# Two of four quarters of a gate stage's input transposed by DMA in 16 bit halves instead of on TensorE

## The chip, the cores and the metric

The kernel runs on one core of a Trainium2 chip. The metric is the device time of one execution in microseconds (us); lower is better. One core has TensorE (PE in the profile: matmuls and transposes into PSUM), VectorE (DVE), ScalarE (ACT), GpSimd (POOL) and SyncE (SP, which only issues transfers here), each with its own instruction stream, and 16 DMA engines that serve all transfers.

## The reference, cut to what matters

One layer of a trunk: sliding window attention, its output projection added to x, then a gate computed from the normed x.

```python
hn = rmsnorm(x, norm_g[0])
y = swa_mixer(hn, w_in, w_out, sinks, rel_bias)   # ends in (out * silu(gate)) @ w_out
x = x + y
emb = p[0] @ ple_proj[0]
g = sigmoid(rmsnorm(x, ple_norm[0]) @ ple_gate[0])
x = x + emb * g
return rmsnorm(x, final_g)
```

Sequence 512, width 2048, float32 throughout; `w_out` and `ple_gate` are 2048x2048, the p input is 512x256.

## The kernel before, in words

The span falls into projections and attention (to 452 us), the w_out stage (452 to 607), the gate stage (607 to about 783) and a short tail. The change is in the last two.

*Products.* Both stages multiply a 512x2048 input by a 2048x2048 weight. Each is cut into 2x2 blocks and done with seven block products instead of eight (1 to 7), at the price of sums and differences: the input's are made on VectorE (`Forms`, L815 to L846), the weight's by accumulating transfers earlier in DRAM (`SUMS`) or, for two products of the gate, in place in SBUF (tiles `grown`, L707). `ORDER_OUT` and `ORDER_PLE` (L649) give the order of the products; w_out's product 2 is itself done by seven smaller products (`small`), whose pieces are put between the others by the tables `SMALL` and `small_steps`. In w_out a product's result is added to or subtracted from blocks of x, which lies in SBUF as `x1s` (`add_y`, `add_to_x`, L1031 and L1033).

*Float32 in three matmuls.* PE multiplies in a reduced format, so each operand is split in a high and a low part and a product takes three matmuls (`mm3`, L126 to L128). The weights come in *pieces* of 128x1024 (512 KB). A piece is loaded by SP (L720) into a tile `braw` or `grown`, split into `bhi` by ScalarE (L727, a cast) and `blo` by VectorE (L728, a subtraction of two SBUF tiles), and used by 12 matmuls, a small product's piece by 6. Splits are made two pieces ahead, loads three to six pieces ahead, in SP's order.

*Turning x.* The gate stage needs x with its columns on the partitions. `turn` (L1005) does it on PE: for a pair of column blocks `kp` and one half of the rows `th`, four transposes of 128x128 by an identity into a PSUM bank (L1015), and two ScalarE multiplications by the norm's gain `pn` from there into the tile `hT` (L1018), of which there are four (`hT0` to `hT3`, each four column blocks by 512 rows). With 8 values of `kp` and two halves there are 64 transposes and 32 multiplications. Twelve of the 16 turns stand in w_out's last product 4, four in the gate's first product 2. A block of x is turned after its last addition (`missing` counts them); at that moment ScalarE also sums its squares (`squares`, L1001) for the norm, whose factor is applied later.

*Order.* Up to the gate's second product a scheduler sets the order of each engine's stream; from there it is as written. Waits are between instructions, and a stream is in order: an instruction that waits holds all that stand behind it on its engine.

Of the kernel before, what the change touches and what calls it, by code (L numbers as in the profile page):

```python
# [11 lines left out]
F32 = mybir.dt.float32  # L12
F32R = mybir.dt.float32r
AF = mybir.ActivationFunctionType
# [4 lines left out]
D = 2048  # L19
# [36 lines left out]
def trunk_kernel(ctx: ExitStack, tc: tile.TileContext, a: dict):  # L56
# [587 lines left out]
    def blk(t):  # L644
# [4 lines left out]
    ORDER_OUT, ORDER_PLE = (1, 7, 6, 5, 3, 4), (2, 7, 1, 6, 5, 3, 4)  # L649

    SMALL = {
        (5, 0): {1: 1, 3: 1}, (5, 1): {1: 7, 3: 7}, (3, 0): {1: 6, 3: 6}, (3, 1): {1: 2, 3: 2},
        (4, 0): {0: 5, 1: 5, 2: 4, 3: 4}, (4, 1): {0: 3, 1: 3},
# [151 lines left out]
    far_from, far_to = at_out[6, 0][0], at_ple[ORDER_PLE[0], 0][0]  # L805

    class Forms:
# [6 lines left out]
        def steps(self, p):  # L814

            self.made[p] = []
            for h in range(2):
# [13 lines left out]
                if sub:  # L831
                    nc.vector.tensor_sub(src, *sub)
                    yield
# [116 lines left out]
    fg = late.tile([P, D], F32, name="fg")  # L950
    pTh = late.tile([P, 2, S], F32R, name="pTh")
    pTl = late.tile([P, 2, S], F32R, name="pTl")
# [5 lines left out]
    def banks(p, jj, nm):  # L958

        if p in (6, 5, 3):  # L960
            return chain[jj]
        tag = ("to" if p in (7, 2) else "sp")[jj]
        ps = [bank(f"{nm}{p}_{jj}_{tb}", tag) for tb in range(2)]
        if p == 1:
            chain[jj] = ps
        return ps

    later = []
# [6 lines left out]
    def unit(p, jj, at, forms, todo, between=lambda m: None):  # L975

        ps = banks(p, jj, forms.nm)
        f = forms.made[p]
        first = p not in (6, 5, 3)
        for m in range(4):  # L980
            bh, bl = B.get(at[p, jj][m])
            for kk in range(2):
# [21 lines left out]

    def turn(kp, th, tag):  # L1005

        g = kp // 2
        if g not in hT:
            hT[g] = quarter(f"hT{g}")
# [6 lines left out]
        for n in range(2):  # L1016
            k = 2 * kp + n
            nc.scalar.mul(hT[g][:, k % 4, th * 256 : th * 256 + 256], tp[:, n * 256 : n * 256 + 256], pn[:, k : k + 1])  # L1018

    ple_forms = Forms(hT, "g")  # L1020
    ple_first = ple_forms.steps(2)


    missing = {(j, t): {(0, 0): 1, (1, 0): 3, (0, 1): 1, (1, 1): 2}[t // 2, j // 2] for j in range(4) for t in range(NB)}
# [3 lines left out]
    def add_to_x(j, t, sign, ps):  # L1028
# [6 lines left out]
        if not missing[j, t]:  # L1035
            squares(t, j)

# [4 lines left out]
    small_forms = {}  # L1042

    def small_form(q):
# [5 lines left out]
        fh, fl = (  # L1050
            acts.tile([P, 2, 256], F32R, tag=tag, name=f"small_{tag}{q}").rearrange("p k (h t) -> p (k h) t", h=2)
            for tag in ("ah", "al")
        )
# [16 lines left out]
        (6, 1, 2): 1, (5, 0, 0): 7, (5, 0, 2): 7, (5, 1, 0): 6, (5, 1, 2): 6, (3, 0, 2): 2, (3, 1, 0): 5, (3, 1, 2): 5,  # L1070
        (3, 1, 3): 4, (4, 0, 1): 3, (4, 0, 3): 3,
# [35 lines left out]
    turns = []  # L1107


# [3 lines left out]
    waiting = {(7, 0): (1, 0), (6, 0): (1, 1)}  # L1113
    held = {}
    for n, p in enumerate(ORDER_OUT):
        nxt = out_forms.steps(ORDER_OUT[n + 1]) if n < 5 else iter(())
        for jj in range(2):
# [11 lines left out]
            def todo():  # L1129
# [19 lines left out]
        if p == 3:  # L1149
            nc.sync.dma_start(fg, a["final_g"].partition_broadcast(P))  # L1150
        if p == 3:
            turns = [(kp, th) for kp0, th in ((4, 1), (4, 0), (0, 0)) for kp in range(kp0, kp0 + 4)]
    run(ple_first)
    assert not turns
# [5 lines left out]
    nc.sync.dma_start(pT, a["pT"])  # L1160
    nc.scalar.copy(pTh, pT)
# [44 lines left out]
    s2, s7 = partial("s2"), partial("s7")  # L1206
# [253 lines left out]
```

## Time and profile before

| What | Value |
|---|---|
| Median of 3 runs | 794.84 us (793.84 to 795.72) |
| The profiled execution | 794.82 us |
| Its span in the trace | 793.1 us |
| Granted TensorE clock | 0.997 |
| PE, DVE, ACT, POOL busy | 783.2, 585.7, 506.7, 148.5 us |
| DMA | 45,066 packets, 185.23 MB |

The profile is of one execution. Its span is what the trace covers; the execution's own time has 1.72 us more around it. A group's row gives the line, the engine, what is written from what, the count, then busy time and the mean duration in ns. A matmul's row shows some 390 ns, while the next starts 227 ns after it, since they are pipelined; the chain of work counts start to start. A row of transfers gives the count, the size and the median time from issue to landing.

### The profile page before, as it was taken

Reading aid. Unit: us, or ns where it says so; the run is one execution under the profiler, and the core shown is the slowest. Engines: PE = TensorE matmul, PEld = TensorE weight load, DVE = VectorE, ACT = ScalarE, POOL = GpSimd, SP = SyncE. Lnnn points to the kernel's source line nnn. Section 1 sums busy time; section 2 is a strip of 40 time slices with the busy share of each in tenths; the row PEclk is TensorE's granted clock in tenths of the full one; section 3 lists DMA queues with packets and bytes.
Section 4 is the critical chain, followed back from the end, with each engine's and each line's share of the span. In section 5 each row is a group of like instructions: output and inputs, shape, how many; then the busy total and the mean of one; then the engine's idle time right before and its main releaser. Section 6 shows DMA issues by size and latency. Waiting matters only on the chain.

```text
span 793.1 us, 11181 instructions
## 1 busy us (share of the span) xinstructions
PE 783.2 (99%) x3746; PEld 656.0 (83%) x3746; DVE 585.7 (74%) x1155; ACT 506.7 (64%) x1067; POOL 148.5 (19%) x248
## 2 busy tenths in 40 slices
PE   9999999999999999999999999999999999999995
PEld 8888888888888888888888888888888888888885
DVE  4547587867867587767777899778866757988896
ACT  6743576666767586766666654466699656656765
POOL 0200423242413324132324200000000120210000
PEclk9999999999999999999999999999999999999998
DMA  9977999897989989898987498667864996787533
GB/s 349 275 215 264 207 275 303 223 267 215 277 227 269 223 249 258 230 247 235 244 227 182 140 365 337 197 212 232 275 237 142 346 203 202 157 225 220 176 107 106
DMA packets 45066, 185.23 MB, mean 234 GB/s; under 512 B 6656, under 2 KB 7680, under 8 KB 39888
## 3 DMA queue, kind: packets, MB, share of 16 engines
q1 hardware_dynamic: 36928, 143.30, 53.0%
q0 software_dynamic: 8080, 41.22, 27.1%
q8 instruction: 29, 0.48, 0.2%
q14 instruction: 29, 0.24, 0.1%
HBM read 177.63 MB, written 62.97 MB: 303 GB/s over the span
## 4 chain that ended last, share of the span: by engine, by line
PE 99%; DVE 0%; ACT 0%; ACTq 0%; issue 0%; DVEq 0%
PE gps L126 7%; PE gps L127 7%; PE gps L128 7%; PE qps L126 7%; PE qps L127 7%; PE qps L128 7%; PE o L127 6%; PE g L128 6%; PE g L127 5%; PE o L126 5%; PE o L128 5%; PE g L126 5%; PE s L477 2%; PE o L583 2%; PE vps L290 2%; PE pt L541 2%
## 5 line engine op out<-in xcount | busy, mean ns | idle before, releaser
L728 DVE TENSOR_TENSOR blo<-braw,bhi 128x1024 fp32r<-128x1024 f32 x102 | 124.4, 1222 | 40.9 <-ACT bhi L727 40.6
L727 ACT CAST bhi<-braw 128x1024 fp32r<-128x1024 f32 x102 | 107.3, 1052 | 72.2 <-PE o L128 24.8
L126 PE MATMUL gps<-xh,whi 128*128 128x512 f32 x256 | 100.0, 390 | 0.0
L127 PE MATMUL gps<-xl,whi 128*128 128x512 f32 x256 | 99.9, 390 | 0.0
L128 PE MATMUL gps<-xh,wlo 128*128 128x512 f32 x256 | 99.8, 390 | 0.0
L126 PE MATMUL qps<-xh,whi 128*128 128x512 f32 x224 | 87.8, 392 | 0.0
L127 PE MATMUL qps<-xl,whi 128*128 128x512 f32 x224 | 87.4, 390 | 0.0
L128 PE MATMUL qps<-xh,wlo 128*128 128x512 f32 x224 | 87.3, 390 | 0.0
L110 DVE TENSOR_TENSOR wlo<-wraw,whi 128x1024 fp32r<-128x1024 f32 x60 | 73.7, 1229 | 6.1 <-ACT whi L109 5.9
L547 DVE TENSOR_TENSOR r<-pt,r 128x256 fp32r<-128x256 f32 x64 | 27.2, 424 | 66.5 <-ACT r L546 65.6
L546 ACT CAST r<-pt 128x256 fp32r<-128x256 f32 x64 | 23.9, 373 | 80.9 <-PE pt L541 80.8
L126 PE MATMUL g<-bhi,fhg 128*128 128x512 f32 x192 | 75.1, 391 | 0.0
L126 PE MATMUL o<-bhi,fho 128*128 128x512 f32 x192 | 74.8, 390 | 0.0
L128 PE MATMUL g<-bhi,flg 128*128 128x512 f32 x192 | 74.8, 389 | 0.0
L127 PE MATMUL o<-blo,fho 128*128 128x512 f32 x192 | 74.8, 389 | 0.0
L128 PE MATMUL o<-bhi,flo 128*128 128x512 f32 x192 | 74.7, 389 | 0.0
L127 PE MATMUL g<-blo,fhg 128*128 128x512 f32 x192 | 74.7, 389 | 0.0
L557 POOL TENSOR_SCALAR_AFFINE_SELECT own<-r 64x512 fp32r<-64x512 f32 (+1 forms) x48 | 32.5, 677 | 224.6 <-DVE r L547 208.7
L109 ACT CAST whi<-wraw 128x1024 fp32r<-128x1024 f32 x60 | 62.2, 1039 | 5.4 <-issue 4.0
L492 POOL COPY t<-sinkb 128x2 f32<-128x2 f32 x64 | 53.2, 839 | 57.7 <-ACT sinkb L873 32.4
L707 POOL DMA_DIRECT2D grown<-in_ple_gate x16 | 13.8, 861 | 231.0 <-DVE blo L728 226.7
L128 PEld LDWEIGHTS gps<-xh,wlo 128*128 128x128 f32 x256 | 48.1, 188 | 10.3
(228 smaller groups left out, 1800.3 us busy)
## 6 DMA issues: line engine op xcount, KB each, us to landing
wraw<-in_w_gate_in SPq DMA_DIRECT2D x32, 512.0 KB, 6.5
w_out<-in_w_out POOLq DMA_DIRECT2D x32, 512.0 KB, 8.0
braw<-w_out SPq DMA_DIRECT2D x32, 512.0 KB, 4.4
wraw<-in_w_q SPq DMA_DIRECT2D x28, 512.0 KB, 5.3
braw<-in_ple_gate SPq DMA_DIRECT2D x24, 512.0 KB, 4.1
braw<-in_w_out SPq DMA_DIRECT2D x22, 512.0 KB, 4.2
xw<-in_first SPq DMA_DIRECT2D x14, 640.5 KB, 6.4
w_out<-in_w_out SPq DMA_DIRECT2D x16, 512.0 KB, 10.1
```

Of the source, the lines that this page charges most:

```text
L109: nc.scalar.copy(hi, raw)
L110: nc.vector.tensor_sub(lo, raw, hi.bitcast(F32))
L126: nc.tensor.matmul(ps, sh, mh, start=first, stop=False, skip_group_check=more)
L127: nc.tensor.matmul(ps, sh, ml, start=False, stop=False, skip_group_check=more)
L128: nc.tensor.matmul(ps, sl, mh, start=False, stop=last, skip_group_check=more)
L290: nc.tensor.matmul(v_ps[t], h[:, c], part_of(high_at, 256, 512), start=f, stop=e, skip_group_check=True)
L492: nc.gpsimd.tensor_copy(two(0, W + W - 1 if late else W, 1), sinkb[:, d : d + 1].unsqueeze(1).to_broadcast([P, 2, 1]))
L546: nc.scalar.copy(rh, src)
L547: nc.vector.tensor_sub(rl, src, rh.bitcast(F32))
L557: nc.gpsimd.affine_select(out=flat(own), in_=flat(r).bitcast(F32), pattern=[[0, 8], [sign, HB]], compare_op=ALU.is_ge, fill=0.0, base=-HB ...
L727: nc.scalar.copy(hi, raw)
L728: nc.vector.tensor_sub(lo, raw, hi.bitcast(F32))
```

## The change

- The two lower quarters of the rows (blocks `t` of 2 and 3, 256 of 512 rows, all columns) are no longer turned on PE. When such a block of x is complete, POOL copies it apart into its 16 bit halves (`apart`), writes them to DRAM (`halves_of`, 256 KB for each of the eight blocks), and some six pieces later (`cross`) SP issues a transposing transfer of 16 bit elements from there into `hT`, where low and high halves fall beside each other again. ScalarE then multiplies by `pn` in place.
- `turn` stays for the upper rows: 8 turns, 32 transposes. Four of them stand in w_out's last product, now 3, and four in the gate's first product, now 7.
- `ORDER_OUT` becomes (1, 7, 4, 6, 5, 3) and `ORDER_PLE` (7, 2, 1, 6, 5, 3, 4). w_out's product 4 accumulates into the banks of product 7 (with 7's sign turned), so that 7 is added to one block of x instead of two. Small products and their forms move with the order.
- The forms of the gate's products are made when the quarters that they need are there (`due`, `forward`, `finish`).
- `fg` (the last norm's gain, 1 MB) and the split p input lie in the tiles that the small products' forms leave, and are loaded later.

```diff
@@
-    ORDER_OUT, ORDER_PLE = (1, 7, 6, 5, 3, 4), (2, 7, 1, 6, 5, 3, 4)
+    ORDER_OUT, ORDER_PLE = (1, 7, 4, 6, 5, 3), (7, 2, 1, 6, 5, 3, 4)
...
-        (5, 0): {1: 1, 3: 1}, (5, 1): {1: 7, 3: 7}, (3, 0): {1: 6, 3: 6}, (3, 1): {1: 2, 3: 2},
...
+        (6, 0): {1: 1, 3: 1}, (6, 1): {0: 7, 2: 7}, (5, 0): {0: 6, 1: 6, 3: 2}, (5, 1): {0: 2, 2: 5, 3: 5},
...
-                        1: (a11, None), 7: (a11, (a21, a11)), 2: (a12, None), 6: (a11, (a22, a11)),
+                        1: (a11, None), 7: (a11, (a11, a21)), 2: (a12, None), 6: (a11, (a22, a11)),
...
-                    nc.vector.tensor_sub(src, *sub)
+                    (nc.vector.tensor_add if (self.nm, p) == ("o", 6) else nc.vector.tensor_sub)(src, *sub)
...
@@
+        if (nm, p) == ("o", 4):
+            return sevens[jj]
...
+    halves_of = [tc.dram_tile([S, 2, 512], U16, name=f"halves_of{j}") for j in range(4)]
...
+    def apart(t, j):
...
+        to = room[:, 1024 * n : 1024 * n + 1024].rearrange("p (h c) -> p h c", h=2)
+        nc.gpsimd.tensor_copy(to, x1[j][:, t, :].bitcast(U16).rearrange("p (c h) -> p h c", h=2))
+        nc.gpsimd.dma_start(halves_of[j][t * P : (t + 1) * P], to)
+        written.append((clock[0], t, j))
+
+    def cross():
+
+        clock[0] += 1
+        while crossed and crossed[0][0] <= clock[0] - 4 and (crossed[0][2] < 2 or clock[0] > 60):
+            _, th, j = crossed.pop(0)
+            for k in range(4):
+                part = hT[j][:, k, th * 256 : th * 256 + 256]
+                nc.scalar.mul(part, part, pn[:, 4 * j + k : 4 * j + k + 1])
+            scaled.add((th, j))
+        while written and written[0][0] <= clock[0] - 6 and (written[0][2] < 2 or clock[0] > 50):
+            _, t, j = written.pop(0)
+            to = turned(j).rearrange("p k t -> p (k t)").bitcast(U16).rearrange("p (k t) -> p k t", k=4)
+            nc.sync.dma_start_transpose(
+                to[:, :, t * 2 * P : (t + 1) * 2 * P], halves_of[j][t * P : (t + 1) * P].rearrange("t h c -> (t h) c")
+            )
...
+    def forward():
+
+        while ahead:
+            p, steps = ahead[0]
+            h = len(ple_forms.made.get(p, ())) // 2
+            if not scaled.issuperset({7: {(0, h), (1, h)}, 2: {(0, 2 + h)}}.get(p, ()) if h < 2 else ()):
+                return
+            if next(steps, "end") != "end":
+                return True
+            ahead.pop(0)
+        return True
...
         if not missing[j, t]:
             squares(t, j)
+            if t >= 2:
+                apart(t, j)
...
-            1: [(c11, -1)], 7: [(c22, 1), (c21, -1)], 6: [(c21, -1)], 5: [(c22, 1)], 3: [(c12, 1)],
+            1: [(c11, -1)], 7: [(c22, -1)], 6: [(c21, -1)], 5: [(c22, 1)], 3: [(c12, 1)],
...
-                if p == 4:
-
-                    for _ in range({0: 1, 1: 2, 2: 2, 3: 2, 5: 1, 6: 2, 7: 2}.get(4 * jj + step, 0)):
-                        turn(*turns.pop(0), "o")
-                    if jj:
-                        next(ple_first, None)
+                cross()
+                if p == 3 and jj:
+                    for kp in {0: (0, 1), 1: (2, 3)}.get(step, ()):
+                        turn(kp, 0, "o")
+                    forward()
...
+    finish()
+    fg = late.tile([P, D], F32, tag="two", name="fg")
+    nc.sync.dma_start(fg, a["final_g"].partition_broadcast(P))
...
+                cross()
+                if p == 7:
+                    for kp in {0: (4,), 1: (5,), 3: (6,), 4: (7,)}.get(4 * jj + step, ()):
+                        turn(kp, 0, "s")
```

Three places in the engines' streams show what has moved. A row there has the line of its kernel (the kernel after has its own numbers: L721 is L720 of before, L1065 is L1018, L1062 is L1015), the operation, and out<-in with the numbers of the tiles.

SP, before, from the end of w_out's loads into the gate stage: the pieces of the gate's product 2 (`braw` from `in_ple_gate`), the p input, and the first seeds of product 7 (`grown` from `ple_gate_7`).

```order
L720 DMA braw61_6181<-w_out_4_1_3_808 128x1024
L720 DMA braw62_6258<-in_ple_gate 128x1024
L720 DMA braw63_6270<-in_ple_gate 128x1024
L720 DMA braw64_6310<-in_ple_gate 128x1024
L1160 DMA pT_6352<-in_pT 128x1024
L720 DMA braw65_6361<-in_ple_gate 128x1024
L720 DMA braw66_6363<-in_ple_gate 128x1024
L720 DMA braw67_6391<-in_ple_gate 128x1024
L720 DMA braw68_6419<-in_ple_gate 128x1024
L720 DMA grown70_6421<-ple_gate_7_0_0_809 128x1024
L720 DMA braw69_6446<-in_ple_gate 128x1024
```

SP, after, at the start of the gate stage: the last seeds of product 7, with `fg` and the p input between them, then the transposing transfers into `hT2` and `hT3`, then the first pieces of product 2.

```order
L721 DMA grown67_6285<-ple_gate_7_1_1_814 128x1024
L1221 DMA fg_6312<-in_final_g 128x2048
L1227 DMA pT_6316<-in_pT 128x1024
L721 DMA grown68_6326<-ple_gate_7_1_2_815 128x1024
L721 DMA grown69_6355<-ple_gate_7_1_3_816 128x1024
L1045 DMA_TRANSPOSE hT2_6352<-halves_of2_5009 128x4x256 x2
L1045 DMA_TRANSPOSE hT3_6401<-halves_of3_5010 128x4x256 x2
L721 DMA braw70_6429<-in_ple_gate 128x1024
L721 DMA braw71_6472<-in_ple_gate 128x1024
```

The weights of product 2 now stand behind four transposing transfers (two in each row with x2), and these behind all seeds of product 7; the other four stand further up, behind the loads of pieces 46, 47, 51 and 52 in w_out's products 5 and 3.

ScalarE, before, in w_out's product 4: casts of pieces (`bhi`), sums of squares (`junk`), and the first evacuations of turned blocks into `hT2` and `hT3`.

```order
L727 CAST bhi49_5991<-braw49_5910 128x1024
L727 CAST bhi50_6006<-braw50_5932 128x1024
L727 CAST bhi51_6035<-braw51_5944 128x1024
L1001 ACTIVATE junk0_0_6023,ssq2_5008<-x1s_5004 128x512
L1018 ACTIVATE hT2_6025<-tp4_1_6026,pn_68 128x256 x2
L727 CAST bhi52_6047<-braw52_5967 128x1024
L1001 ACTIVATE junk3_0_6064,ssq2_5008<-x1s_5004 128x512
L727 CAST bhi53_6086<-braw53_5989 128x1024
L1018 ACTIVATE hT2_6025<-tp5_1_6066,pn_68 128x256 x2
L1018 ACTIVATE hT3_6073<-tp6_1_6074,pn_68 128x256 x2
L727 CAST bhi54_6098<-braw54_6004 128x1024
```

ScalarE, after, over pieces 42 to 47 in w_out's products 5 and 3: the in-place multiplications of `hT0` and `hT1` (L1040), which need the transposing transfers landed.

```order
L728 CAST bhi42_5841<-braw42_5762 128x1024
L1040 ACTIVATE hT0_5862<-hT0_5862,pn_68 128x256 x4
L728 CAST bhi43_5866<-braw43_5786 128x1024
L728 CAST bhi44_5889<-braw44_5798 128x1024
L1006 ACTIVATE junk2_2_5918,ssq2_5005<-x1s_5004 128x512
L728 CAST bhi45_5901<-braw45_5827 128x1024
L728 CAST bhi46_5931<-braw46_5839 128x1024
L728 CAST bhi47_5943<-braw47_5864 128x1024
L1136 CAST small_two3_6028<-small_sums_5011 128x512
L1040 ACTIVATE hT1_5966<-hT1_5966,pn_68 128x256
L1006 ACTIVATE junk0_0_5960,ssq2_5005<-x1s_5004 128x512
L1006 ACTIVATE junk2_3_5987,ssq2_5005<-x1s_5004 128x512
```

The four multiplications of `hT0` stand ahead of the cast of piece 43. Of those of `hT1`, the first comes ahead of the cast of piece 48 and the other three between the casts of 48 and 49.

POOL, after, behind the loads of x; before, the accumulations of `grown` (L707 there, L708 here) followed at once.

```order
L999 DMA x1s_5004<-in_x 128x4x512 x2
L1029 COPY apart0_5698<-x1s_5004 128x1024 x2
L1030 DMA halves_of0_5007<-apart0_5698 128x1024 x2
L1029 COPY apart0_5698<-x1s_5004 128x1024
L1030 DMA halves_of1_5008<-apart0_5698 128x1024
L1029 COPY apart0_5698<-x1s_5004 128x1024
L1030 DMA halves_of1_5008<-apart0_5698 128x1024
L1029 COPY apart4_5920<-x1s_5004 128x1024 x2
L1030 DMA halves_of2_5009<-apart4_5920 128x1024 x2
L1029 COPY apart4_5920<-x1s_5004 128x1024 x2
L1030 DMA halves_of3_5010<-apart4_5920 128x1024 x2
L708 DMA grown62_6150<-in_ple_gate 128x1024
```

Eight copies and eight writes now stand between the loads of x and the first accumulation.

More of the change, by code (lines that the diff above doesn't have):

```diff
@@ L1049, in small_form @@
         }[q]
[L1050 to L1053, printed above, removed]
+        tag, n = {1: ("one", 0), 7: ("one", 1), 6: ("two", 0), 2: ("two", 1), 5: ("one", 0), 4: ("one", 1), 3: ("two", 0)}[q]
+        if n == 0:
+            pairs[tag] = late.tile([P, 4, 512], F32R, tag=tag, name=f"small_{tag}{q}")
+        fh, fl = (pairs[tag][:, 2 * n + v].rearrange("p (k t) -> p k t", k=4) for v in range(2))
         small_forms[q] = fh, fl
@@ L1148, in trunk_kernel @@
         run(nxt)
[L1149 to L1154, printed above, removed]
+        if p == 5:
+            due(7)
+    finish()
+    fg = late.tile([P, D], F32, tag="two", name="fg")
+    nc.sync.dma_start(fg, a["final_g"].partition_broadcast(P))
     rstd2 = const.tile([P, NB], F32, name="rstd2")
@@ L1160, in trunk_kernel @@
     nc.sync.dma_start(pT, a["pT"])
+    pTs = late.tile([P, 2, 2, S], F32R, tag="one", name="pTs")
+    pTh, pTl = pTs[:, 0], pTs[:, 1]
     nc.scalar.copy(pTh, pT)
@@ L1290, in trunk_kernel @@
                 later.extend(moved.pop())
[L1291 removed]
+        if p != 7:
+            finish()
     while later:
```

85 lines of the change are left out of this document (53 added, 32 removed).

## The prediction

> **What bounds the kernel now.** I read the page first: the busy shares and the chain that ended last.
>
> ```profile
> PE 783.2 (99%) x3746; PEld 656.0 (83%) x3746; DVE 585.7 (74%) x1155; ACT 506.7 (64%) x1067; POOL 148.5 (19%) x248
> PE 99%; DVE 0%; ACT 0%; ACTq 0%; issue 0%; DVEq 0%
> ```
>
> TensorE is busy for 99% of the span and is 99% of the chain. An average can hide a stage with another limit, so next came the windows of the stages that the change touches (columns: PE, PEld, DVE, ACT, POOL busy, clock, DMA share, GB/s).
>
> ```profile
> 470.00:480.00 10.00, 10.00 (x45) 8.16 (x44) 10.00 (x12) 5.56 (x7) 0.00 (x0) 1.00 0.72 257
> 490.00:500.00 10.00, 10.00 (x45) 8.26 (x44) 8.71 (x11) 5.77 (x7) 0.00 (x0) 1.00 0.83 312
> 500.00:510.00 10.00, 10.00 (x46) 8.28 (x45) 6.14 (x7) 3.67 (x4) 0.00 (x0) 1.00 0.63 206
> 585.00:590.00 5.00, 5.00 (x29) 4.24 (x28) 3.15 (x4) 4.04 (x8) 0.00 (x0) 1.00 0.99 393
> 590.00:600.00 10.00, 10.00 (x50) 8.30 (x49) 8.96 (x11) 9.50 (x18) 0.00 (x0) 1.00 0.03 12
> 640.00:650.00 10.00, 10.00 (x46) 8.29 (x45) 5.50 (x5) 5.20 (x7) 2.79 (x4) 1.00 1.03 192
> ```
>
> PE has no gap in any of them, at full clock. So every microsecond taken off PE here comes off the end, if nothing makes PE wait; and every wait of PE is added in full. Three neighbours are close: VectorE is full at 470-480 (and eases to 6.14 of 10 by 510), ScalarE nearly so at 590-600, and the DMA engines are full at 585-590 and at 640-650. The last two differ: at 585-590 plain loads move 393 GB/s, at 640-650 a full set of engines moves 192, because only the accumulating transfers of `grown` run then.
>
> The pace of a piece of weights shows in those accumulations, each released by the split of one piece:
>
> ```profile
> 636.66 0.85 POOL L707 DMA_DIRECT2D grown<-in_ple_gate  x1 [1.87 <-DVE blo L728]
> 639.38 0.85 POOL L707 DMA_DIRECT2D grown<-in_ple_gate  x1 [1.87 <-DVE blo L728]
> ```
>
> A piece is 2.72 us of PE, and one accumulation takes that long with all engines busy.
>
> **What it removes.** Half of the 64 TensorE transposes go. The chain's longest pieces price them (start, length, what):
>
> ```profile
> 574.97 0.44 PE tp L1015 x4
> 579.53 0.87 PE tp L1015 x8
> ...
> 606.75 0.87 PE tp L1015 x8
> 610.37 0.44 PE tp L1015 x4
> 613.56 0.44 PE tp L1015 x4
> ...
> 619.95 0.44 PE tp L1015 x4
> ```
>
> There are six pieces of 4 (0.44) and five of 8 (0.87): 2.64 + 4.35 = 6.99 us for 64. What stays is two groups of 8 and four of 4: 1.74 + 1.76 = 3.50. So PE loses 6.99 - 3.50 = 3.49 us. The count of matmuls is otherwise the same: product 4 accumulates in the banks of product 7, which costs PE nothing. The bound from below is 794.82 (this execution, span 793.1 and 1.72 around it) - 3.49 = 791.33.
>
> ```profile
> L1018 ACT ACTIVATE hT<-tp,pn 128x256 f32<-128x256 f32 x32 | 12.8, 472 | 0.0
> L1033 DVE TENSOR_TENSOR x1s<-x1s,o 128x512 f32<-128x512 f32 x12 | 7.8, 681 | 0.0
> L728 DVE TENSOR_TENSOR blo<-braw,bhi 128x1024 fp32r<-128x1024 f32 x102 | 124.4, 1222 | 40.9 <-ACT bhi L727 40.6
> L727 ACT CAST bhi<-braw 128x1024 fp32r<-128x1024 f32 x102 | 107.3, 1052 | 72.2 <-PE o L128 24.8 <-PE g L128 20.0 <-DMA braw<-w_out 7.5
> ```
>
> ScalarE's 32 multiplications become 16 from PSUM and 16 in place, of the same 128x256: no change in sum. VectorE loses four additions into x, 4 x 0.68 = 2.7 us, because product 7 goes to one block of x instead of two. Nothing of this is on the chain, so it counts nothing. The new order does move VectorE's sums and additions earlier, into the full stretch that begins at 470, by some 1 us around the sixteenth piece (the changed order, summed with these durations); a wait of PE there is under 1 us, and from 490 on VectorE has the room to make it up.
>
> **What it adds on POOL.** Eight copies to 16 bit halves and eight writes of 256 KB, on an engine that does nothing in the windows from 470 to 600; behind them on POOL stand only the accumulations of `grown`, first due at the end of the w_out stage. For the copies the nearest row of the engine is the masking of 128x512.
>
> ```profile
> 110.11 0.67 POOL L557 TENSOR_SCALAR_AFFINE_SELECT own<-r 128x512 fp32r<-128x512 f32 x1 [4.58 <-DVE r L547]
> 105.34 0.18 POOL L492 COPY t<-sinkb 128x2 f32<-128x2 f32 x1
> 111.24 1.46 POOL L492 COPY t<-sinkb 128x2 f32<-128x2 f32 x1
> 111.45 1.23 DVE L110 TENSOR_TENSOR wlo<-wraw,whi 128x1024 fp32r<-128x1024 f32 x1
> x1s<-s POOLq DMA_DIRECT2D x4, 256.0 KB, 5.2
> ```
>
> For 1,024 halves that is 2 x 0.67 = 1.3 us by elements. The transposes are issued six pieces (16 us) behind the writes, and copy and write are 1.3 + 5.2 = 6.5 us, so their length is covered. What isn't: the small copy took 0.18 us alone and 1.46 us when a VectorE split of two SBUF inputs started 0.21 us in; it ended only with the split. So POOL waits for VectorE, and I must suppose the reverse: each copy can hold a split back by up to 1.3 us. A split comes 2 pieces ahead, so one delay is absorbed where VectorE has room; in a full stretch it isn't. The bounds are 0 and 8 x 1.3 = 10.4 us; I take 0.3, a quarter of one copy, since the copies begin past 500, where VectorE has room. The Trainium skill, "SBUF — State Buffer", § Who interferes with whom, holds that a VectorE instruction with two SBUF inputs and a GpSimd one that reads SBUF shut each other out for a whole instruction, whichever began first; by that the copies' price would be near the upper bound in a full stretch. The trace agrees in the one direction that it shows (1.46 against 0.18), and no row shows the other.
>
> **What it adds on SP: eight DMA transposes of 256 KB.** No row of before shows one. Call T the time for which one holds the DMA engines. From the nearest rows:
>
> ```profile
> out<-x1s SPq DMA_DIRECT2D x14, 256.0 KB, 2.8
> braw<-in_ple_gate SPq DMA_DIRECT2D x24, 512.0 KB, 4.1
> q1 hardware_dynamic: 36928, 143.30, 53.0%
> ```
>
> At the rate of plain loads (393 GB/s) T is 256 KB / 393 = 0.67 us. The far end: SP's queue took 0.53 x 16 x 793.1 / 36,928 = 0.182 us of an engine for each packet (3.9 KB in the mean); if each run of 256 bytes were a packet, 1,024 of them on 16 engines would take 64 x 0.182 = 11.7 us. I take the first, since the data is the same and the row of 256 KB, landing in 2.8 us, is the nearest in size; both ends stay for the range.
>
> They come in three groups. *The two of hT0* stand on SP behind the loads of pieces 46 and 47, and ScalarE's four multiplications stand ahead of the cast of piece 43: from issue to need about two pieces, 5.4 us, against 2.8 to 4.1 for landing. *The two of hT1* likewise before pieces 48 and 49. For T = 0.67 both are hidden, and up to T about 2.
>
> *The four of hT2 and hT3* are the tight place. SP reaches them behind the last seed, and the first waits for ScalarE's evacuation of the sixth TensorE turn, in the gate's product 7. Behind it on SP are the weights of product 2, pieces 70 and on. Counted from the start of product 7, that turn ends after two pieces and two groups of 4 (5.4 + 0.9), and ScalarE needs some 1.5 us (two multiplications of 0.47 and half a cast of 1.05, as an estimate): 7.8 us. Product 2 starts at 8 x 2.72 + 4 x 0.44 = 23.5, and its first piece must be on chip for the split (1.05 + 1.22, with the handovers some 2.4) before: 21.1. That leaves 13.3 us for four transposes and one load. Meanwhile the accumulations run, one for each 2.72 us. What a load costs beside them:
>
> ```profile
> L720 SPq DMA_DIRECT2D braw<-ple_gate x3: 319/319/320, 675.9 to 704.4; - x3
> DMA to landing us min/median/max: 3.3/6.3/8.0
> 695.00:700.00 5.00, 5.00 (x23) 4.14 (x23) 4.42 (x6) 2.47 (x4) 1.72 (x2) 1.00 1.03 171
> ```
>
> Among accumulations (window 674 to 705) a load landed in up to 8.0 us where alone it takes 4.1. So I give SP's queue half of the engines: 4 x 2T, then the load's 2 x 1.33 and 3 us that landing takes beyond transfer (4.1 - 1.33 = 2.8): 8T + 5.7. With T = 0.67 that is 11.1, inside 13.3. The point at which PE waits is 8T = 7.6, T = 0.95. Beyond it the stall is 8T - 7.6.
>
> **What moves.** Product 7 leads the gate stage, so that it needs only the turned quarters hT0 and hT1 at its start; fg (1 MB) and the p input are loaded between the last seeds. The cast of p stands on ScalarE ahead of the cast of piece 63.
>
> ```profile
> 583.74 0.70 SPq L1160 DMA_DIRECT2D pT<-in_pT  x1
> 599.82 9.63 SPq L720 DMA_DIRECT2D braw<-in_ple_gate  x4
> fg<-in_final_g SPq DMA_DIRECT2D x1, 1024.0 KB, 5.9
> ```
>
> SP sends nothing between 584 and 599 before, and the window 590-600 shows the DMA engines at 0.03: here there is room for 1.5 MB (4 us at 393 GB/s), with loads running up to six pieces ahead. I price it at nothing; without that cover it is at most 5.9 us once. The sum: 794.82 - 3.49 + 0.3 = 791.6.
>
> **The rivals.** *1. The transposes run at about half rate.* T of 1.2 to 1.6 gives stalls of 8T - 7.6 = 2 to 5.2 us at the start of product 2: the time is 793.3 to 796.5, 795 in the middle, no difference that can be told (a measurement of this kernel tells 0.2%, 1.6 us). For it: its runs are of 128 halves, 256 bytes, a sixteenth of the queue's mean packet. Against: the row of 256 KB, which is the same amount of data. Chance 0.15.
>
> *2. The transposes are slow, and product 2 waits for its weights.* Past T = 1.6 the kernel is slower by more than 0.2%. At T = 3 the stall is 16.4 us, and 791.3 + 16.4 = 807.7; at T = 2 it is 8.4, and the time 799.7. For it: the far end of T by packets is 11.7 us, and SP's queue is in order, so that one slow transfer delays all the weights behind. Against: nothing but the nearness of the 256 KB row. Chance 0.25. A rule of the Trainium skill, "VectorE: DVE Perf Modes", § Rules for kernel authors, speaks for this rival: transpose 128x128 on TensorE if PSUM will do. Its § The three transpose paths has 1,309 ns for a 128x128 of 16 bits by DMA; eight such blocks one after another would be an estimated T of 10.5 us. Against this "Advanced Engine Details and Errata", § X-Bar Transpose (TRN2), says that "TRN2 transpose DMAs are as fast as regular DMAs", which would be the T that I took. No row here decides between them.
>
> *3. POOL's copies hold VectorE.* If each of the eight copies delays a split by its 1.3 us where there is no room, PE waits up to 10 us; where half of that is absorbed, 5 us, at pieces 25 to 50: 791.3 + 5 = 796.3. For it: the two copies above. Against: two pieces of lead, and the 6.14 to 8.96 of 10 that VectorE shows after 490. Chance 0.10, of it 0.02 faster, 0.04 in between, 0.04 slower.
>
> **How the numbers follow.** The forecast has 0.50, its own range being 790.4 to 793.2 (0.9 under the bound for the spread of runs, up to the edge of faster). Faster: 0.50 + 0.02 = 0.52; same: 0.15 + 0.04 = 0.19; slower: 0.25 + 0.04 = 0.29. The median of the runs of before, 794.84, is the profiled time but for 0.02, so that the sum stands for both. The range reaches from 790.4 to 800, which holds the forecast, rivals 1 and 3 and of rival 2 the part up to T = 2 (0.07): 0.82. Past T = 2 lies the far end, T = 11.7, at 8 x 11.7 - 7.6 = 86 us of stall for this group alone: it is left out.
>
> **What would show it.** Right: 32 transposes on the PE in six pieces of the chain, 3.5 us in all; PE windows without a gap from 470 to 650; the DMA transposes landing in about 3 us, those of hT2 and hT3 and the next load of weights within 13 us. Wrong: idle PE before the first matmul of the gate's product 2, released by a split whose cast waited for a load behind the transposes (rivals 1 and 2); a cast of piece 43 or 49 behind late multiplications on ScalarE; copies on POOL with a split stretched to 2.5 us beside them (rival 3).

## The result and the profile after

The changed kernel takes 805.65 us in the median of 4 runs (800.40 to 808.04), before on the same chip 794.70: a ratio of 1.0133, 95% interval 1.0105 to 1.0161. It is slower by 11 us, where 3 us faster was forecast. The profiled execution is the fastest of the four, 800.40 us (span 798.7), so the trace shows half of the loss. The other three runs take 5 to 8 us more, and there is no trace of those.

The page's busy shares and its chain, after:

```profile
PE 783.4 (98%) x3714; PEld 652.3 (82%) x3714; DVE 586.3 (73%) x1151; ACT 507.7 (64%) x1067; POOL 164.6 (21%) x264
PE 88%; DVE 5%; DMA 2%; ACT 2%; issue 1%; SPq 1%; ACTq 0%; DVEq 0%
```

TensorE has 32 instructions fewer, as it should. But the chain, 99% PE before, now runs through VectorE, ScalarE, the DMA engines and SP as well. The windows tell where PE waits (columns as before; the first figure behind the length is PE's busy time):

```profile
470.00:480.00 10.00, 9.71 (x44) 7.70 (x43) 10.00 (x13) 5.20 (x7) 0.00 (x0) 1.00 0.69 233
560.00:570.00 10.00, 8.39 (x34) 6.29 (x35) 9.45 (x9) 5.70 (x8) 4.04 (x4) 1.00 0.88 222
570.00:580.00 10.00, 8.89 (x39) 6.79 (x38) 5.34 (x6) 7.61 (x13) 1.09 (x2) 1.00 0.80 294
620.00:630.00 10.00, 8.42 (x39) 6.44 (x38) 1.93 (x3) 1.96 (x4) 1.70 (x2) 0.96 1.16 242
630.00:640.00 10.00, 9.13 (x33) 6.68 (x33) 7.10 (x8) 8.90 (x15) 0.86 (x1) 0.87 1.05 305
```

There are three places: 476, 560 to 576, and 626 to 635. Matmuls follow each other at 0.227 us. What their starts are further apart than that sums to 0.45, 3.8 and 4.9 us, 9.2 in all. With the 3.49 us of transposes that went, 794.82 - 3.49 + 9.2 = 800.5 against 800.40: the trace closes. The last place, in TensorE's own rows:

```profile
626.02 0.39 PE L129 MATMUL g<-bhi,flg 128*128 128x512 f32 x1
627.23 0.49 PE L127 MATMUL g<-bhi,fhg 128*128 128x512 f32 x1 [0.81 <-ACT bhi L728]
628.48 0.50 PE L128 MATMUL g<-blo,fhg 128*128 128x512 f32 x1 [0.76 <-DVE blo L729]
...
629.77 0.63 PE L129 MATMUL g<-bhi,flg 128*128 128x512 f32 x1
630.20 0.63 PE L127 MATMUL g<-bhi,fhg 128*128 128x512 f32 x1
```

PE waits twice for the split of a piece (for its high part, then for its low part), and behind these waits the matmuls are 0.43 us apart instead of 0.227. The weights are those of product 7, which were on chip already. What held their cast is in ScalarE's rows, at 625 and 630, and at 558 and 571 for the second place:

```profile
557.82 1.71 ACT L1040 ACTIVATE hT<-hT,pn 128x256 f32<-128x256 f32 x4 [3.83 <-DMA hT<-halves_of]
571.03 0.51 ACT L1040 ACTIVATE hT<-hT,pn 128x256 f32<-128x256 f32 x1 [3.45 <-DMA hT<-halves_of]
625.61 0.62 ACT L845 CAST fhg<-hT 128x512 fp32r<-128x512 f32 x1 [5.59 <-DMA hT<-halves_of]
630.01 0.47 ACT L1065 ACTIVATE hT<-tp,pn 128x256 f32<-128x256 f32 x1 [2.46 <-DMA hT<-halves_of]
```

Each time ScalarE stands idle for a transposing transfer, and the casts stand behind. At 625 it is the form of product 2, which reads only the *upper* rows of hT2; the transfer writes the *lower* ones. At 630 it is the evacuation of a TensorE turn into the upper rows of hT3. In hT upper and lower rows lie interleaved, column block by column block, so the wait was set although no byte is shared (e7_halves below, with the two apart, has neither wait). SP and the landing of the eight transposes:

```profile
551.71 1.29 SPq L1045 DMA_TRANSPOSE hT<-halves_of  x1
564.96 1.23 SPq L1045 DMA_TRANSPOSE hT<-halves_of  x1
616.33 9.54 SPq L1045 DMA_TRANSPOSE hT<-halves_of  x4
625.92 24.75 SPq L721 DMA_DIRECT2D braw<-in_ple_gate  x11
```

```profile
L1045 SPq DMA_TRANSPOSE hT<-halves_of x8: 1232/1394/3432, 547.8 to 624.4; - x8
DMA to landing us min/median/max: 4.2/6.4/8.3
```

SP itself is busy for 1.2 to 3.4 us with the issue of one transpose, against 0.3 to 0.4 for a load, and they land after 4.2 to 8.3 us, not 2.8 to 4.1. The lead of hT0 and hT1 is far shorter than forecast, too: SP issues the second transpose of hT0 at 551.71, and ScalarE has reached its multiplications at 557.82 - 3.83 = 553.99, which is 2.3 us later and not 5.4; for hT1 it is 2.6 us (564.96 to 571.03 - 3.45). Last, two copies on POOL and the VectorE split beside the second, each in its engine's rows, then the group of all splits:

```profile
546.29 1.99 POOL L1029 COPY apart<-x1s 128x1024 uint16<-128x1024 uint16 x1 [12.09 <-DVE x1s L1103]
549.11 1.05 POOL L1029 COPY apart<-x1s 128x1024 uint16<-128x1024 uint16 x1
```

```profile
548.75 2.50 DVE L729 TENSOR_TENSOR blo<-braw,bhi 128x1024 fp32r<-128x1024 f32 x1
```

```profile
L729 DVE TENSOR_TENSOR blo<-braw,bhi 128x1024 fp32r<-128x1024 f32 x102 | 127.5, 1257 | 46.2 <-ACT bhi L728 46.1
```

The split of 1.22 us took 2.50 while a copy of 1.05 ran in it. The other copy, begun 0.14 us into a split (546.15), took 1.99. Over all 102 splits it is 127.5 us, 3.1 more than before.

### The profile page after: what moved, and what is told of

It is laid out like the page before. It is cut to its first block, busy times and chain, and to the rows that moved or that the text cites. A ratio compares the mean times of both kernels' runs of the same rounds, so it can differ in the third digit from the quotient of the medians.

```text
span 798.7 us, 11162 instructions
## 1 busy us (share of the span) xinstructions
PE 783.4 (98%) x3714; PEld 652.3 (82%) x3714; DVE 586.3 (73%) x1151; ACT 507.7 (64%) x1067; POOL 164.6 (21%) x264
## 3 DMA queue, kind: packets, MB, share of 16 engines
q1 hardware_dynamic: 45376, 145.40, 54.3%
## 4 chain that ended last, share of the span: by engine, by line
PE 88%; DVE 5%; DMA 2%; ACT 2%; issue 1%; SPq 1%; ACTq 0%; DVEq 0%
PE qps L127 7%; PE qps L128 7%; PE qps L129 7%; PE gps L127 7%; PE gps L128 7%; PE gps L129 7%; PE g L128 5%; PE g L127 5%; PE g L129 5%; PE o L128 4%; PE o L129 4%; PE o L127 4%; DVE blo L729 2%; PE s L478 2%; PE vps L291 2%; PE o L584 2%
## 5 line engine op out<-in xcount | busy, mean ns | idle before, releaser
L729 DVE TENSOR_TENSOR blo<-braw,bhi 128x1024 fp32r<-128x1024 f32 x102 | 127.5, 1257 | 46.2 <-ACT bhi L728 46.1
L127 PEld LDWEIGHTS gps<-xh,whi 128*128 128x128 f32 x256 | 48.1, 188 | 9.1
```

The source lines that it names most:

```text
L127: nc.tensor.matmul(ps, sh, mh, start=first, stop=False, skip_group_check=more)
L729: nc.vector.tensor_sub(lo, raw, hi.bitcast(F32))
```

## The experiments

Theory: the waits come from where the transposes stand, in streams that are in order; in the gate stage it is ScalarE's wait that nothing needs. Rivals: the transposing itself is slow; POOL's copies lock VectorE; the new order costs. Each kernel was timed beside the kernel before on the same chip (its medians: 794.68, 794.47, 794.42 and 794.27 in the four groups).

| Run | Median, us | Ratio to before, 95% interval |
|---|---|---|
| e2_plain | 803.53 | 1.0105 (1.0077 to 1.0134) |
| e3_nocopy | 806.71 | 1.0149 (1.0133 to 1.0166) |
| e4_both | 800.48 | 1.0070 (1.0053 to 1.0086) |
| e7_halves | 822.97 | 1.0349 (1.0310 to 1.0388) |
| e5_order | 795.37 | 1.0015 (1.0006 to 1.0024) |
| e6_late | 795.74 | 1.0019 (1.0011 to 1.0028) |
| e9_two | 795.95 | 1.0021 (1.0012 to 1.0030) |
| e10_act | 794.69 | 1.0003 (0.9995 to 1.0012) |
| e11_hold | 792.12 | 0.9969 (0.9957 to 0.9980) |
| e12_hold_act | 791.28 | 0.9963 (0.9950 to 0.9977) |
| e14_quiet, e15_busy | 793.98, 793.84 | one run each |
| e13_same_place | 809.74 | 1.0219 (1.0156 to 1.0281) |
| e16_weights_first | 818.50 | 1.0285 (1.0248 to 1.0321) |

### First group: the suspects one by one

**e2_plain**

```diff
-        nc.gpsimd.dma_start(halves_of[j][t * P : (t + 1) * P], to)
+        nc.gpsimd.dma_start(
+            halves_of[j][t * P : (t + 1) * P].rearrange("t h c -> t (h c)"), x1[j][:, t, :].bitcast(U16)
+        )
...
-            nc.sync.dma_start_transpose(
...
+            nc.sync.dma_start(
...
```

> In place of each transposing transfer a plain one of the same 256 KB; the copies on POOL are still made, but what is written is x as it is, so the lower halves of hT hold x untransposed. If the transposing itself is what costs (1.6 us of the DMA engines and 1.2 to 3.4 us of SP for each, against 0.67 and 0.35), the median falls from 805 to 796-799, both the wait of 5 us at the gate's product 7 and that at hT0 going down to under 1 us each. If the copies on POOL cost most, by locking VectorE, it stays at 803 or more. If it is the place of the waits on ScalarE, it falls by a third or half, since a plain transfer lands about 3 us sooner.

803.53: of the 11 us only 2 go, and the two intervals overlap. By the number alone this is also the case "the copies on POOL cost most" (803 or more); e4_both takes that up. In the trace, ScalarE waits in the same places for plain transfers. In the gate stage SP issues the four from 614.64 on, and they land 5.7 to 11 us after their issue, the last at 627.8:

```profile
621.24 0.62 ACT L845 CAST fhg<-hT 128x512 fp32r<-128x512 f32 x1 [4.17 <-DMA hT<-halves_of]
627.88 0.47 ACT L1068 ACTIVATE hT<-tp,pn 128x256 f32<-128x256 f32 x1 [4.22 <-DMA hT<-halves_of]
```

So in the gate stage it is the place, more than the transposing: PE loses no less there than in the changed kernel. At 558 ScalarE still waits 2.6 us, for transfers that land after 5.2.

**e3_nocopy**

```diff
-        nc.gpsimd.tensor_copy(to, x1[j][:, t, :].bitcast(U16).rearrange("p (c h) -> p h c", h=2))
...
+            nc.gpsimd.memset(room.bitcast(F32), 1.0019302368164062)
```

> The eight copies on POOL are left out: what is written to DRAM, and then transposed, is a constant from a tile that is set twice. If the copies lock VectorE, no split should be longer than 1.3 us any more, and the waits of PE between 559 and 576 (3.8 us in the profile) shrink to under 2; the median falls by 2 to 4 us, to 801-803. If the transposes alone make those waits, the splits go back to 1.22 us and the median stays within 1.5 us of 805.

The splits go back to 1,222 ns: the copies do hold VectorE. The waits at 565 and 577 go down to 0.8 us, but e10_act below has no copies on POOL either and keeps them, so that this isn't shown to be the copies. The median is 806.71, which neither expectation had. In part that is the edit's own fault: a constant needs no x, so all eight writes went out at 459.5 and met the loads of weights and of x at the head of the stage, where PE now waits 4.6 us and runs at half pace behind that. The gate stage is slower as well, PE loses some 12 us there instead of 5, and this run doesn't show why. The writes on POOL, the late cast on ScalarE, and the group of splits:

```profile
459.50 4.31 POOL L1030 DMA_DIRECT2D halves_of<-apart  x8
```

```profile
473.14 1.04 ACT L728 CAST bhi<-braw 128x1024 fp32r<-128x1024 f32 x1 [6.80 <-DMA braw<-in_w_out]
```

```profile
L729 DVE TENSOR_TENSOR blo<-braw,bhi 128x1024 fp32r<-128x1024 f32 x102 | 124.2, 1222 | 53.4 <-ACT bhi L728 53.0
```

**e4_both** is both edits without the constant: x is written as it is, and no copy is made.

> Neither copies nor transposes: x is written as it is by POOL and read back by plain transfers (the lower halves of hT hold x untransposed). The order of the products, the adds and the 32 transposes on PE are as in the changed kernel. If the order of products costs nothing but the 0.45 us at 476, this is the forecast's case, 791.5 to 793. If the order or the waits' place costs, it stays above 795.

800.48, 8.6 us over what the new order by itself would give (795.37 - 3.49, e5_order below). Against e2_plain, which has the copies, it is 3 us less. ScalarE still waits 6.5 us for plain transfers before the form of product 2. Neither suspect is the main cause.

**e7_halves**

```diff
-            hT[g] = quarter(f"hT{g}")
+            hT[g] = quarter(f"hT{g}").rearrange("p k t -> p (k t)").rearrange("p (h k t) -> p h k t", h=2, k=4)
...
```

The other lines of the edit only follow the new layout.

> Only the layout of hT is changed: the upper and the lower 256 rows lie one behind the other instead of interleaved for each column block. The forms of product 2 read the upper ones alone, and with this layout they have no wait for the transposes of the lower ones, nor have those to wait for the turned upper ones. If that needless wait is the cause at the gate's product 7, the 5 us there vanish, and the median falls by 5 to 9 us, to 796-800, still above before because of the waits at hT0 and hT1. If the weights of product 2 behind the transposes on SP are the cause, the wait only moves to product 2, and the median stays over 802.

822.97: the wait only moves to product 2, as in the second expectation, but it is far longer than the one that went. ScalarE's wait is gone, and so is what had held the transposes back to 616. They now go out at 602.7, into the accumulations, and SP needs 24 us to issue four; they land after 11 to 32 us, and PE waits 18 us for the first piece of product 2. The accumulations land after 11 to 22 us; in e6_late below, where they run beside plain loads, after 8 to 10. SP's rows, then ScalarE's cast of that piece:

```profile
602.69 24.34 SPq L1046 DMA_TRANSPOSE hT<-halves_of  x4
627.09 32.93 SPq L721 DMA_DIRECT2D braw<-in_ple_gate  x8
```

```profile
650.46 2.24 ACT L728 CAST bhi<-braw 128x1024 fp32r<-128x1024 f32 x2 [23.18 <-DMA braw<-in_ple_gate]
```

The needless wait is thus not the whole cause: the run changes the place of the transposes along with the wait. What transposes and accumulations do to each other had to be seen apart.

### Second group: the place, the order, the copies

**e5_order** takes the copies, writes and transfers out and turns the lower rows on TensorE too, in products 3 and 2.

```diff
-            if t >= 2:
-                apart(t, j)
...
+                elif p == 3:
+                    turn(step, 1, "o")
...
+                if (p, jj) == (2, 1):
+                    turn(4 + step, 1, "s")
```

> The changed kernel's order of products and adds, with all 64 transposes on TensorE and no copies, no writes and no transposing transfers. If the order alone costs what the run without copies and transposes still shows at 476 and 572 (0.8 + 1.0 us), the median is 796 to 797. If it costs nothing by itself, it is 794.7, as before.

795.37: the order costs 0.9 us (ratio 1.0006 to 1.0024), with waits of 0.7 us at 476 and 0.4 at 653 in the trace. That is between the two expectations, and small.

**e6_late**

```diff
-        while written and written[0][0] <= clock[0] - 6 and (written[0][2] < 2 or clock[0] > 50):
+        while written and written[0][0] <= clock[0] - 6 and (written[0][2] < 2 or clock[0] > 60):
```

> Only the threshold is moved from which the four transposes of hT2 and hT3 are issued: from step 50 to step 60, behind the forms of product 2 and behind the loads of its weights, when the first eight accumulations are through. If the wait of product 7's casts behind those transposes is the cause of the wait at 626-634, that vanishes (4.9 us in the profile, more in the timed runs), and the median falls from 805 to 796-798, the waits of the w_out stage being left. If the transposes are slow wherever they stand, the wait comes back at product 6, which needs them, or at the weights behind them, and the median stays over 801.

One number, and 795.74 instead of 805.65. PE has no wait after 576. The four transposes now go out at 641, behind the first eight accumulations and the forms of product 2, and land in 3.4 to 5.2 us:

```profile
641.16 6.62 SPq L1045 DMA_TRANSPOSE hT<-halves_of  x4
```

What is left is the wait of 2.1 us at 560, with 1.6 us at half pace behind it, and 0.5 us each at 476 and 575.

**e9_two** keeps the transposes of hT0 and hT1 only.

```diff
-                apart(t, j)
+            if t >= 2 and j < 2:
+                apart(t, j)
...
+                if (p, jj) == (2, 1):
+                    turn(4 + step, 1, "s")
```

> The four transposes of hT2 and hT3 and their copies and writes are replaced by 16 more transposes on TensorE in the gate's product 2; those of hT0 and hT1 stay with DMA. If only the gate stage's transposes cost, the median is 794.7 - 1.75 + 2 (the waits of the w_out stage less half of the copies): about 795 to 797. If the transposes of hT0 and hT1 cost as much, it is over 799.

795.95, as expected for a cost that is in the gate stage: 794.47 - 1.75 and 2.8 us of waits in the trace make 795.5.

**e10_act** is e6_late with

```diff
-        nc.gpsimd.tensor_copy(to, x1[j][:, t, :].bitcast(U16).rearrange("p (c h) -> p h c", h=2))
+        nc.scalar.copy(to, x1[j][:, t, :].bitcast(U16).rearrange("p (c h) -> p h c", h=2))
```

> As the run with the late transposes, and in addition the eight copies are made by ScalarE instead of POOL. If POOL's copies hold VectorE (splits of 2.06 and 2.50 us in the changed kernel), no split is longer than 1.3 us, the waits of PE at 560-576 shrink from 3.8 to under 1.5 us, and the median is 1 to 2.5 us below that run, at or below before. If the casts of pieces suffer from the copies on ScalarE in their place (eight of some 1 us), it stays the same or gets slower.

794.69, 1 us less, which is the time expected if the copies hold VectorE. But the waits at 560 to 576 are still 4.0 us: it is not the copies that make them.

### Third group: holding ScalarE's multiplications, and one transpose by itself

**e11_hold** is e6_late, and the multiplications of hT0 and hT1 read a gain that depends on a later block:

```diff
-        while crossed and crossed[0][0] <= clock[0] - 4 and (crossed[0][2] < 2 or clock[0] > 60):
+        while crossed and crossed[0][0] <= clock[0] - 4 and not missing[{0: (2, 3), 1: (0, 1)}.get(crossed[0][2], (2, 3))]:
...
+                pnl = const.tile([P, KC], F32, name=f"pn_late{j}")
+                nc.vector.scalar_tensor_tensor(
+                    out=pnl, in0=pn, scalar=ssq2[:, tb, jb : jb + 1], in1=pn, op0=ALU.min, op1=ALU.max
+                )
...
-                nc.scalar.mul(part, part, pn[:, 4 * j + k : 4 * j + k + 1])
+                nc.scalar.mul(part, part, pnl[:, 4 * j + k : 4 * j + k + 1])
```

> As the run with the late transposes, and ScalarE's in-place multiplications of hT0 and hT1 are held back by a made dependence (their gain goes through one small VectorE instruction that reads a later sum of squares), to behind the casts of pieces 48 and 57 instead of 42 and 47. If the wait of PE at 560 (1.1 + 1.0 us and what follows it) comes from multiplications that wait on ScalarE for late transposes, it vanishes, and the median falls by 2 to 4 us from 795.7, to 792-794. If it comes from POOL's copies alone, the wait stays, and the median with it.

792.12. The wait at 560 is gone; ScalarE finds the data there (the row has no wait in front):

```profile
568.51 1.71 ACT L1047 ACTIVATE hT<-hT,pn_late 128x256 f32<-128x256 f32 x4
```

**e12_hold_act** is that with the copies on ScalarE.

> As the run before it, and the copies are made by ScalarE. If POOL's copies still hold VectorE's splits, this takes 0.5 to 1.5 us more off: 791.5 to 793. If the copies on ScalarE delay casts, it is the same or up to 1 us slower.

791.28, 0.4% under before (0.9950 to 0.9977) and 0.3 us from the forecast. Here is the whole change with three things mended: the transposes of hT2 and hT3 are issued later, the multiplications of hT0 and hT1 are held back, and the copies are off POOL. The splits are back at 124.5 us, and PE's wait is as small as before:

```profile
PE 779.2 (99%) x3714; PEld 651.8 (83%) x3714; DVE 583.6 (74%) x1153; ACT 516.0 (65%) x1075; POOL 153.0 (19%) x256
```

```profile
L729 DVE TENSOR_TENSOR blo<-braw,bhi 128x1024 fp32r<-128x1024 f32 x102 | 124.5, 1223 | 44.4 <-ACT bhi L728 43.8
```

**e14_quiet** and **e15_busy** put four transposes (256 KB each, from x, for nobody) into the kernel before. In e14_quiet they stand behind the load of the p input; in e15_busy at the start of the second half of product 7.

```diff
     nc.sync.dma_start(pT, a["pT"])
+    probe()
```

> The kernel before, with four transposing transfers of 256 KB (from the input x into a tile that nothing reads) issued behind the load of the p input at 584, when the DMA engines soon go idle (0.03 from 590 to 600). It shows what one costs by itself. At the rate of plain loads four take 4 x 0.67 = 2.7 us of the engines and some 1.4 us of SP; at the 1.6 us that the packets of the changed kernel suggest, 6.5 us; if SP's issue of 1.2 to 1.4 us each is the limit, they follow each other at that pace. The time stays within 0.5 us of before, since SP waits there anyway.

With the loads drained by about 592, what moves is the transposes alone (windows; the last two columns are the DMA share and GB/s):

```profile
592.00:594.00 2.00, 2.00 (x10) 1.66 (x9) 1.83 (x3) 2.00 (x5) 0.00 (x0) 1.00 1.33 191
594.00:596.00 2.00, 2.00 (x10) 1.65 (x10) 1.14 (x2) 2.00 (x5) 0.00 (x0) 1.00 1.33 97
596.00:598.00 2.00, 2.00 (x11) 1.60 (x10) 2.00 (x3) 1.62 (x2) 0.00 (x0) 1.00 0.58 130
```

From 592 to the last landing at 597.4 that is (191 + 97 + 130) x 2 us = 0.84 MB in 5.4 us, 155 GB/s: four in a row have a T of 1.7 us each, two and a half times the 0.67 of a plain load, with the DMA engines full up to 596. The pages of before and after agree, by an estimate: SP's queue has 45,376 packets after and 36,928 before, 1,056 more for each of the eight transposes, and 54.3% against 53.0% of 16 engines' span is 214 us more, 0.025 us for a packet and 1.7 us of all engines for a transpose.

> The same four transposes, issued in the kernel before behind the last seed of product 7 (617), so that they and the loads behind them meet the accumulations from 628 on. If transposes beside accumulations are no slower than loads (up to 8 us for landing), the four are through within 10 us and the time stays within 1 us. If they slow each other as the run with the new layout of hT suggests (24 us for four issues, 118 to 176 GB/s), the issues take over 2 us each and the loads behind them land after 10 us or more; PE waits for product 1's weights, and the time rises by 2 to 15 us.

Inconclusive: the transposes were issued by 627.1 and landed by 631, so that only the first of the accumulations (from 627.9) ran beside them. PE waited for nothing.

### Fourth group: the two causes of the gate stage apart

**e13_same_place** is e7_halves with a hold:

```diff
+            if (t, j) == (2, 2):
+                nc.scalar.copy(turned(2)[:, 1, 0, 0:1], turned(2)[:, 0, 3, 255:256])
```

> The layout of hT with the lower rows apart, so that the casts of product 2's forms and the evacuations into hT3 don't wait for the transposes; but a one-column copy on ScalarE, behind the sixth turn, holds the four transposes back to the place that they have in the changed kernel (616). If ScalarE's needless wait is the whole cause at 626-634, PE has no wait there and the median is near that of the run with the late transposes, 796. If the weights of product 2, which stand on SP behind the four transposes, come too late as well (issued at 626, on chip not before 630, where PE would need them split at 628), PE waits for the first cast of product 2 instead, by 5 us or more, and the median stays at 801 or more.

809.74 in the median: ScalarE's needless wait is gone and nothing is won, as the second expectation had it. The profiled execution is the slowest of the four by 9 us (819.89, the others 808.80 to 810.60), so its figures are the far end. There SP reaches the transposes at 622 (the execution is 4.3 us late by then, and the hold is 1.6 us later than the wait that it replaces), and the load behind them comes so late that PE waits 18.5 us for product 2. In these windows PE's work runs out, and the DMA engines are full of next to nothing:

```profile
632.00:636.00 4.00, 2.72 (x13) 1.91 (x11) 0.00 (x0) 0.00 (x0) 0.00 (x0) 1.00 1.45 150
636.00:640.00 4.00, 0.00 (x0) 0.00 (x0) 0.00 (x0) 0.00 (x0) 0.00 (x0) 0.81 1.29 46
640.00:644.00 4.00, 0.00 (x0) 0.00 (x0) 0.00 (x0) 0.00 (x0) 0.00 (x0) 0.50 1.21 67
```

**e16_weights_first** is e7_halves with step 54 instead of 50.

> The same layout, no hold, and the transposes stand on SP behind the first three pieces of product 2 (step 54 instead of 50). If only what stands behind the transposes on SP is late, the wait moves on to the fourth piece and shrinks to under 8 us: 797 to 804. If the transposes and the accumulations slow each other whatever the order, the pieces behind them are late by 10 us or more and the median is over 805.

818.50, the second expectation. Three pieces are ahead now, and the fourth is 19 us late: the order on SP only moves the wait. SP needs 51 us for four issues.

```profile
605.63 51.18 SPq L1046 DMA_TRANSPOSE hT<-halves_of  x4
```

Why the changed kernel lost only 11 us can be read in POOL's rows of its trace, though no run shows it by itself: an accumulation is released by a split, and ScalarE's needless wait held the splits.

```profile
621.16 0.85 POOL L708 DMA_DIRECT2D grown<-in_ple_gate  x1 [3.19 <-issue]
628.72 0.85 POOL L708 DMA_DIRECT2D grown<-in_ple_gate  x1 [6.72 <-DVE blo L729]
634.49 0.86 POOL L708 DMA_DIRECT2D grown<-in_ple_gate  x1 [4.91 <-DVE blo L729]
```

While ScalarE stood, from 620.0 to 625.6, no split was made, no accumulation was issued between 621.2 and 628.7, and the transposes landed by 630. Without that wait both stay in the engines together (e7, e13, e16).

## Why the prediction was wrong

The forecast was a sum with two covers in it: transposes that land before anyone needs them cost nothing. Both covers failed. The trace has 3.8 us of PE's waits where the first should have held and 4.9 where the second should have, and with both mended the forecast's time came.

- **Half of the turns off TensorE: right.** 32 transposes went, and where nothing else stands in the way the time falls by what they took: 794.42 - 791.28 = 3.1 us in e12_hold_act, against 3.49.
- **"11.1, inside 13.3": the step that failed, for hT2 and hT3.** The sum counted one wait only, that of product 2 for its weights behind the transposes on SP. In the changed kernel ScalarE waited first, 5.6 and 2.5 us, for the tile that the transposes write, with the casts of product 7 behind it in its stream. I priced what is queued behind the transposes on SP, and not who waits for their tile. Issued later, the same transposes cost PE nothing there, and the time falls by 10 us (e6_late).
- **The 11.1 itself: mis-sized in both its parts.** T is 1.7 us in a row of four and not 0.67; "the data is the same" was no argument. The far end of T had the number of packets about right (1,024, by the pages 1,056) and their price wrong, 0.025 us and not 0.182. With 1.7, 8T + 5.7 is 19.3, a stall of 6 and a time of 797. "Half of the engines" was too much as well: even four plain transfers (e2_plain) took 13.2 us from the first issue to the last landing, where 8 x 0.67 + 2.8 gives 8.2. Where nothing holds the accumulations back it is far worse: four transposes took SP 13 to 51 us, and the engines, full, moved 46 to 150 GB/s (e13, e7, e16).
- **"From issue to need about two pieces, 5.4 us": wrong, for hT0 and hT1.** The trace has 2.3 and 2.6 us for the second transpose of each, and landing takes 6.0. So "hidden up to T about 2" fails with plain transfers too: in e2_plain they land after 5.2 us and ScalarE waits 2.6. Holding the multiplications back takes 3.6 us off (e6_late to e11_hold).
- **Rival 2: half right.** It had slow transposes and the weights of product 2 late behind them; e7, e13 and e16 show that wait. That its 807.7 lies near the measured 805.65 is luck: it is for T = 3, and in the changed kernel the wait was another.
- **Rival 3: right in kind, small in time.** A split was stretched to 2.50 us, as the list of signs has it. Taking the copies off POOL is worth 1.0 us (e6_late to e10_act) and 0.8 (e11_hold to e12_hold_act, whose intervals overlap), where I took 0.3. The new order costs 0.9 (e5), of the size that I gave for VectorE's full stretch (under 1) and left out of the sum.

What stays open: why transposes and accumulations slow each other so far; the only run that was to show it by itself, e15_busy, is inconclusive. Open, too, is what the 5 us are which the timed runs of the changed kernel have over the profiled one. They went with the late transposes (e6_late: 795.74, profiled 796.28).

## What to carry to other kernels

Before work is moved to a transfer, ask for each engine in order what stands behind the instruction that will wait for it, and for which bytes it really waits: a tile whose halves are written by two engines should have them apart. Taking such a wait away is only safe when one knows what it held back. And a transfer of a new kind has no price from one of an old kind, alone or in company: measure it once in an idle window, and keep it out of the windows where the DMA engines are full. Last, a lead is read from rows, as the time from the issue to the moment at which the waiting engine is free, and not counted in pieces.

## What the runs showed of the hardware

- Four transposing transfers in a row, 256 KB each of 16 bit elements, moved 155 GB/s with nothing beside them (e14_quiet), where plain loads move 393 GB/s (before, 585 to 590). The Trainium skill, "Advanced Engine Details and Errata", § X-Bar Transpose (TRN2), has them as fast as plain ones; these runs don't agree.
- Their issue kept SP busy for 1.2 us or more each, against 0.3 to 0.4 for a load.
- Among accumulating transfers four of them kept SP for 13 to 51 us (e13, e7, e16), and the engines moved 46 to 150 GB/s at a share of 1.1 to 1.45 (e13).
- A copy on POOL that reads SBUF and a VectorE subtraction of two SBUF tiles shut each other out in both directions: 2.50 us against 1.22 for the split, 1.99 against 1.05 for the copy. The Trainium skill, "SBUF — State Buffer", § Who interferes with whom, says so; the trace now agrees both ways.
- After two waits of 2.0 us in sum (626 to 628.5), matmuls ran 0.43 us apart for 3 us, at a granted clock of 0.50; after those at 560 in the same trace (1.8 us) they did not. The length of the waits alone doesn't decide it: in e10_act waits of 2.6 us (560.4 to 563.5) left the clock at 1.00.
